# A hybrid gMLP and dilated-attention block: another order of the units in each half of the input projection

## Chip, cores and metric

One core of one Trainium2 chip. The metric is the device time of one execution in microseconds (us); every time below is a median of runs or a row of one profiled execution.

## The reference

`x` has 2048 tokens of 1024 features, in fp32. It is normalised and projected to nine groups of 1024 columns (gate_logits is two), which feed two branches:

```python
h = rmsnorm(x, g_norm)
proj = h @ w_in
a_u, a_v, a_gate, q, k, v, b_gate, gate_logits = jnp.split(proj, splits, axis=-1)
y_a = chunked_spatial_gating(gelu(a_u), gelu(a_v), w_s, b_s, g_v) * silu(a_gate)
y_b = dilated_attention(q, k, v) * silu(b_gate)
g_a, g_b = jnp.split(sigmoid(gate_logits), 2, axis=-1)
merged = g_a * (y_a @ w_proj_a) + g_b * (y_b @ w_proj_b)
return rmsnorm(x + merged @ w_out, g_final)
```

Column groups are told here by short names: u, av, g (branch A: a_u, a_v, a_gate), k, q, v, bg (b_gate), ga and gb (the two halves of gate_logits).

## The kernel before

**Precision.** Each fp32 operand is split in a high part (a cast, fp32r) and a low part (the rest, fp32r), and each product of a tile is three matmuls: hi x hi, hi x lo, lo x hi (`mm3`, L103). For weights ACT makes the high part (L83) and, from the end of the first V unit on, POOL the low part (L86); for the input ACT makes the high part (L144) and DVE or POOL the low part (L145).

**Halves and quarters.** Tokens are handled in two halves (`hf`) of 1024, each of two quarters (`qd`) of 512. X is the split, normalised input, 8 chunks of 128 features per quarter. `stats(qd)` (L155) loads 4 blocks of rows of x into two buffers ("xr", L161), squares and sums them on ACT (L162), scales on DVE (L77), takes the power -0.5 on POOL (L78), spreads the result over all partitions with four matmuls (L167), and ACT copies it to `rsbc` (L170). `h_chunk` (L147) then loads a chunk of x transposed and multiplies it by `rsbc` on DVE (L151). Four buffers ("ht") hold such chunks.

**Seven products.** Most units multiply blocks of a half as a 2 x 2 matrix with seven products (Strassen). They need input differences: T1 to T3 (`make_T`, L186: three loaded chunks, three DVE differences L196 to L200, the low parts on POOL) and T4 (`make_T4`, L204: DVE L212 and L213). T4 lies where part of X lay; `restore` makes that part again, from new loads. Weights go through a ring of 8 buffers; raw weights have two buffers.

**Units.** `unit_rows` is V of the first half; `ev_v` empties its banks (POOL fills ones, L447; ACT L451; DVE L452; a DMA). `unit_SR` makes outputs by rows (v of the second half and av): 2 blocks of weights x 7 products x 2 banks of 24 matmuls of 128x256. `unit_S` makes outputs by columns (k, q, u, g, bg, ga): 4 blocks of weights x 7 products of 12 matmuls of 128x512. `unit_P` is a plain product for one quarter, 8 banks of 24 matmuls of 128x512 (gb). `branch_a` runs u and g in turn.

**Scales.** k and q are stored in fp16 with a scale per group of columns. `scales_ahead` (L251) is a generator: 16 steps, each with a load of 128x1024 weights (`wrow`, in the "xr" buffers) and a DVE reduce (L262, with a running maximum, L265); then POOL's `partition_all_reduce` (L269) and three DVE steps. Calls of `next` set between which pieces of work it stands.

**Order.** A scheduler takes the program's text as priority and places each instruction on its engine's queue when its own model says that it is ready; each engine then runs its queue in order, and DMAs are issued from SP's. So a piece of text further down can stand earlier on an engine. First half: X of quarter 0, V, X of quarter 1 within V, T, T4, av with the scales among it, k, q, u and g, then bg, ga, restore. Second half: gate unit P0 on the old half's quarter 0 (still in X), X of quarter 2, statistics of quarter 3, gate unit P1 (old quarter 1), restore, T, T4, v, av, k, q, u, g, restore. Attention and the projections follow and are not touched.

Of the kernel before, what the change touches and what calls it, by code (L numbers as in the profile page):

```python
# [27 lines left out]
class Prog:  # L28
# [141 lines left out]
        nc.scalar.copy(bc, ps)  # L170
        self.bc[qd % 2] = bc

    def make_h(self, hp, qd):
        self.stats(hp, qd)
        X = self.alloc_X(qd % 2)
        for k in range(KC):
            self.split_X(X, k, self.h_chunk(hp, "ht", 4, qd, k))
        return X
# [568 lines left out]
    def window(self, at, fill, total_fill):  # L747
# [35 lines left out]
        for j in range(n + 3):  # L783
            if j < n:
                G = groups[j]
                h, p, g = G["h"], G["p"], G["g"]
                if g == 3 and j + 1 < n:
                    q = j // 4 + 1
                    vt[q // 3, 2 - q % 3] = self.load_v(at, q // 3, 2 - q % 3)
                if g == 0:  # L790
                    if p == 2:
                        OC = at.tile([P, 3, 16, 66], F32, name="OC", tag="OC", bufs=1)
                    if p == 1 and h + 1 < NH:
                        raw[h + 1] = self.load_qk(at, h + 1)
                if g == 0:
                    O = OC[:, 0] if p == 0 else at.tile([P, 16, 66], F32, name="ob", tag="ob", bufs=2)
                G.update(qk=self.qkp[p] if p else raw[h][:3], B=raw[h][3], V=vt[h, p], OC=OC, O=O)
                run(self.stage_s(at, G))

                nxt = {2: (h, 1), 0: (h + 1, 2)}.get(p)  # L800
                if nxt and nxt[0] < NH and g == 0:
                    perm = self.permuted(at, raw[nxt[0]], nxt[1])
                next(perm, None)
            if 2 <= j < n + 2:
                run(self.stage_t(at, groups[j - 2]))
            if j >= 3:
                G = groups[j - 3]
                run(self.stage_o(at, G))
                if G["p"] == 0 and G["g"] == 3:
                    pend.append(self.combine(at, G["h"], G["OC"]))  # L810
# [98 lines left out]
    def run(self):  # L909
        tc, io = self.tc, self.io  # L910
        self.setup()
        win = io["w_in"]
        self.pe = None

        def drain(g):
            for _ in g:
                pass
        self.bc = [None, None]

        def pool(name, **kw):  # L920
            return tc.tile_pool(name=name, **kw)
        with pool("tp", bufs=1) as self.tp, pool("wr", bufs=2) as self.wr, pool("cp", bufs=1) as self.cp:
            X = [None, None]
            for hf in range(2):
                qds = (2 * hf, 2 * hf + 1)
                with pool(f"hp{hf}", bufs=2) as hp:
                    rows = self.ev_v(hp, hf)
                    if hf == 0:
                        X[0] = self.make_h(hp, 0)
                        gen = self.unit_rows(X, win, 5120, rows, (0, 1), lambda wb: self.sv[:, wb:wb + 1])  # L930
                        next(gen)
                        X[1] = self.make_h(hp, 1)
                        drain(gen)
                        self.w_lo = self.nc.gpsimd
                    else:
                        drain(self.unit_P(X, win, 8192, self.ev_gate(self.gb_d), 0))
                        X0 = self.make_h(hp, 2)
                        self.stats(hp, 3)
                        drain(self.unit_P(X, win, 8192, self.ev_gate(self.gb_d), 1))
                        X = [X0, [None] * KC]  # L940
                        self.restore(X, 3, range(4, KC))
                    self.make_T(hp, qds)
                    self.make_T4(X)
                    if hf == 1:
                        drain(self.unit_SR(hp, X, win, 5120, rows))
                    ahead = self.scales_ahead(hp, win, (4096, 3072)) if hf == 0 else iter(())
                    for _ in self.unit_SR(hp, X, win, 1024, self.ev_av(hf)):
                        next(ahead, None)
                    drain(ahead)
                    if hf == 0:  # L950
                        self.scales()
                with pool(f"wq{hf}", bufs=2) as self.wq:
                    branch_a = self.branch_a(self.wq, hf, X)
                    next(branch_a)
                    for c0, dst, sc in ((4096, self.k_d, self.sk), (3072, self.q_d, self.sq)):
                        drain(self.unit_S(X, win, c0, self.ev_qk(dst, sc), qds))
                    drain(branch_a)
                if hf == 0:
                    drain(self.unit_S(X, win, 6144, self.ev_bg, qds))
                    drain(self.unit_S(X, win, 7168, self.ev_gate(self.ga_d), qds))  # L960
                self.restore(X, qds[1])
        self.wp = self.ctx.enter_context(pool("wp", bufs=2))
        self.every = 8
        self.w_hi = self.nc.gpsimd
        self.x_lo = self.nc.vector

        def fill():
            e = self.every
            yield from self.unit_T(X, win, 6144, self.ev_bg, (2, 3), every=e)
            yield from self.unit_T(X, win, 7168, self.ev_gate(self.ga_d), (2, 3), every=e)  # L970
            Y = [None, None]
            yield from self.unit_T(X, win, 8192, self.ev_gate(self.gb_d), (2,), every=e)
            Y[0] = self.load_X(0, self.ya_d)
            yield from self.unit_T(X, win, 8192, self.ev_gate(self.gb_d), (3,), every=e)
            for qd in range(4):
                if qd < 3:
                    Y[(qd + 1) % 2] = self.load_X(qd + 1, self.ya_d)
                yield from self.unit_T(Y, io["w_proj_a"], 0, self.ev_pa, (qd,), every=e)
        with tc.tile_pool(name="at", bufs=2) as at:
            self.window(at, fill(), 80 * 5.2)  # L980
        self.final()
# [48 lines left out]
```

## Time and profile before

| | |
|---|---|
| median of 3 runs | 2685.8 us (2683.05 to 2686.45) |
| the profiled execution's own time | 2690.79 us |
| its span in the trace | 2688.8 us |
| its mean granted TensorE clock | 0.974 |
| bg, ga and P0 (second half's first gate unit) | from about 560 to 758 us of the span |
| the first V unit's end, T4 and av's start | from about 100 to 200 us |
| the second V unit | from about 803 us |

A span is the time from the first to the last instruction in the trace; some 2 us of the run lie around it. In the rows further down, PE is TensorE's matmuls, PEld its weight loads, DVE VectorE, ACT ScalarE, POOL GpSimd and SP the engine that issues DMAs. "x12" counts instructions that a row holds together. An arrow "out<-in" names the tiles; wch and wcl are the two parts of a weight, wc both in one tile, pj, pt and ss are PSUM banks.

### The profile page before, as it was taken

What the parts mean: (1) busy time and instruction counts of PE and PEld (TensorE: products, weight loads), DVE (VectorE), ACT (ScalarE), POOL (GpSimd) and SP (SyncE); (2) the same over time, 40 slices, a digit from 0 to 9 for tenths busy, and PEclk for the clock granted to TensorE, in tenths of its full rate; (3) what the DMA queues carried; (4) which work ended last, traced back from release to release, by engine and by line L of the source; (5) the groups of instructions that cost most, each with busy time, mean ns of one, the idle gap of its engine ahead of it and who ended that gap; (6) DMA issues with size and microseconds to landing.
All of it is one profiled execution on the core that took longest, in us unless ns stands there. A gap on an engine that the chain in (4) does not pass through costs nothing.

```text
span 2688.8 us, 45128 instructions
## 1 busy us (share of the span) xinstructions
PE 2503.2 (93%) x16736; PEld 2122.7 (79%) x16736; DVE 1794.8 (67%) x3633; ACT 1255.1 (47%) x2481; POOL 888.2 (33%) x633
## 2 busy tenths in 40 slices
PE   5969999999998999999899899989889898899998
PEld 5969888888887898888677778878777777677787
DVE  5864767756258547677457877787989888545533
ACT  4335333343333353333257777676767665222221
POOL 0325554444444444544222222333333333000000
PEclk9989999999999999999899999999999999999999
DMA  7744333253453343323356646677777876755541
GB/s 232 162 126 142 102 118 106 94 171 116 153 167 89 87 138 115 122 95 114 99 142 158 185 127 181 177 195 201 200 217 194 237 206 176 239 168 184 169 132 63
DMA packets 463995, 410.00 MB, mean 152 GB/s; under 512 B 150432, under 2 KB 384288, under 8 KB 463776
## 3 DMA queue, kind: packets, MB, share of 16 engines
q1 hardware_dynamic: 463344, 407.05, 51.7%
q8 instruction: 132, 2.16, 0.3%
q14 instruction: 87, 0.71, 0.1%
q10 hardware_dynamic: 432, 0.07, 0.0%
HBM read 297.35 MB, written 109.71 MB: 151 GB/s over the span
## 4 chain that ended last, share of the span: by engine, by line
PE 67%; DVE 13%; DMA 10%; issue 4%; ACT 3%; POOL 1%; SPq 0%; ACTq 0%; DVEq 0%; POOLq 0%
PE pj L103 32%; PE pt L103 15%; PE ss L103 10%; PE pt L669 3%; DVE S L647 2%; PE ss L639 2%; DVE pl L673 1%; DVE X L145 1%; PE ss L640 1%; DMA v_d<-vst 1%; DMA wraw<-in_w_in 1%; DMA OC<-o_d 1%; DMA o_d<-ob 1%; PE pt L512 1%; DVE OC L727 1%
## 5 line engine op out<-in xcount | busy, mean ns | idle before, releaser
L103 PE MATMUL pj<-X,whi 128*128 128x512 f32 x1792 | 602.3, 411 | 16.5 <-POOL whi L85 11.1
L86 POOL TENSOR_TENSOR wc<-wraw,wc 128x512 fp32r<-128x512 f32 x240 | 327.4, 1372 | 318.7 <-ACT wc L83 307.2
L103 PEld LDWEIGHTS pj<-X,whi 128*128 128x128 f32 x1792 | 342.5, 195 | 88.1 <-POOL whi L85 12.0
L103 PE MATMUL pj<-X,wlo 128*128 128x512 f32 x896 | 369.2, 412 | 7.6 <-DVE wlo L86 4.0
L647 DVE CUSTOM_DVE_ANT_0 S<-ss,B,niqk 128x256 f32<-128x256 f32 (+1 forms) x768 | 284.3, 418 | 22.0 <-PE ss L640 21.8
L673 DVE SCALAR_TENSOR_TENSOR pl<-pt,ph 128x512 f16<-128x512 f32 x320 | 204.8, 653 | 93.3 <-ACT ph L672 92.0
L653 ACT ACTIVATE S<-S,ob 128x128 f32<-128x128 f32 (+1 forms) x512 | 193.4, 437 | 72.5 <-DVE ob L647 71.5
L83 ACT CAST wc<-wraw 128x512 fp32r<-128x512 f32 x240 | 145.2, 618 | 165.3 <-PE pt L103 78.8
L85 POOL TENSOR_SCALAR whi<-wraw 128x1024 fp32r<-128x1024 f32 x64 | 69.9, 1093 | 442.9 <-PE pj L103 393.2
L103 PEld LDWEIGHTS pj<-X,wlo 128*128 128x128 f32 x896 | 175.1, 195 | 46.5 <-DVE wlo L86 6.9
L672 ACT ACTIVATE ph<-pt 128x512 f16<-128x512 f32 x320 | 177.2, 565 | 61.1 <-PE pt L669 37.0
L103 PE MATMUL ss<-T,wc 128*128 128x512 f32 x768 | 188.2, 394 | 0.0
L103 PE MATMUL pt<-X,wc 128*128 128x512 f32 x768 | 185.2, 390 | 0.0
L103 PE MATMUL pj<-WO,X 128*128 128x512 f32 x768 | 180.7, 395 | 4.1 <-ACT X L872 3.9
L103 PEld LDWEIGHTS pj<-WO,X 128*128 128x128 f32 x768 | 144.2, 188 | 40.0 <-ACT X L872 5.2
L669 PE MATMUL pt<-ident,S 128*128 128x128 f32 x1200 | 168.6, 278 | 3.4 <-DVE pl L673 3.3
L86 POOL TENSOR_TENSOR wcl<-wraw,wch 128x1024 fp32r<-128x1024 f32 x52 | 129.2, 2486 | 121.4 <-ACT wch L83 97.2
L103 PEld LDWEIGHTS ss<-T,wc 128*128 128x128 f32 x768 | 143.6, 188 | 32.0
L103 PEld LDWEIGHTS pt<-X,wc 128*128 128x128 f32 x768 | 143.9, 188 | 30.3
L86 POOL TENSOR_TENSOR wlo<-wraw,whi 128x1024 fp32r<-128x1024 f32 x64 | 164.5, 2571 | 5.3
L103 PE MATMUL pt<-T,wc 128*128 128x512 f32 x672 | 165.0, 394 | 0.0
L669 PEld LDWEIGHTS pt<-ident,S 128*128 128x128 f32 x1200 | 141.7, 144 | 15.1 <-DVE pl L673 4.4
(229 smaller groups left out, 5777.8 us busy)
## 6 DMA issues: line engine op xcount, KB each, us to landing
wraw<-in_w_in SPq DMA_DIRECT2D x64, 1024.0 KB, 5.7
V<-v_d SPq DMA_DIRECT2D x48, 520.0 KB, 4.8
o_d<-ob SPq DMA_DIRECT2D x32, 528.0 KB, 5.1
OC<-o_d SPq DMA_DIRECT2D x32, 528.0 KB, 4.7
wraw<-in_w_in SPq DMA_DIRECT2D x32, 512.0 KB, 5.4
wraw<-in_w_proj_a SPq DMA_DIRECT2D x32, 512.0 KB, 5.3
wraw<-in_w_proj_b SPq DMA_DIRECT2D x32, 512.0 KB, 4.7
xt<-in_xT SPq DMA_DIRECT2D x60, 256.0 KB, 4.3
```

Source lines behind the costliest of these rows:

```text
L83: nc.scalar.copy(hi, raw)
L85: nc.gpsimd.tensor_scalar(out=hi, in0=raw, scalar1=1.0, scalar2=0.0, op0=ALU.mult, op1=ALU.add)
L86: self.w_lo.tensor_tensor(out=lo, in0=raw, in1=hi.bitcast(F32), op=ALU.subtract)
L103: self.pe = nc.tensor.matmul(out, st(a, k), mv(b, k), start=first and n == 0, stop=last and n == len(todo) - 1)
L145: self.x_lo.tensor_tensor(out=X[k][1], in0=src, in1=X[k][0].bitcast(F32), op=ALU.subtract)
L512: nc.tensor.matmul(px[:, i * P:(i + 1) * P], av[:, 4 * q + i], w, start=True, stop=True)
L639: nc.tensor.matmul(ps[:, i, :n], q, KH[:, w], start=True, stop=False)
L647: nc.vector.tensor_tensor_reduce(out=S[:, j, :n], in0=ps[:, i, :n], in1=B[:, bo:bo + n], scale=self.niqk[:, pr:pr + 1], scalar=3e38, op0=A ...
L653: nc.scalar.activation(S[:, i, :rng[i]], S[:, i, :rng[i]], AF.Exp, bias=ob[:, i, 65:66], scale=-1.0)
L669: self.pe = nc.tensor.transpose(px[:, j * P:(j + 1) * P], G["S"][:, i, c * P:(c + 1) * P], self.ident)
L672: nc.scalar.activation(ph[:, :n], px[:, :n], AF.Copy, scale=PSCALE)
L673: nc.vector.scalar_tensor_tensor(out=pl[:, :n], in0=px[:, :n], scalar=PSCALE, in1=ph[:, :n], op0=ALU.mult, op1=ALU.subtract)
```

## The change

bg and ga of the first half, which stood behind g, now stand ahead of av, right behind T4, and the text puts two steps of the scales behind each of their eight blocks. In the second half the text makes the statistics of quarter 2 ahead of P0, those of quarter 3 and the differences T behind it, and X of quarter 2 behind T (`make_h` is told not to make the statistics again); T4 is behind restore as before. The V unit of the second half now stands in the `else` arm.

```diff
-    def make_h(self, hp, qd):
-        self.stats(hp, qd)
+    def make_h(self, hp, qd, have=False):
+        if not have:
+            self.stats(hp, qd)
...
                         drain(gen)
                         self.w_lo = self.nc.gpsimd
+                        self.make_T(hp, qds)
+                        self.make_T4(X)
+                        ahead = self.scales_ahead(hp, win, (4096, 3072))
+                        for c0, ev in ((6144, self.ev_bg), (7168, self.ev_gate(self.ga_d))):
+                            for _ in self.unit_S(X, win, c0, ev, qds):
+                                next(ahead, None)
+                                next(ahead, None)
+                        drain(ahead)
                     else:
+                        self.stats(hp, 2)
                         drain(self.unit_P(X, win, 8192, self.ev_gate(self.gb_d), 0))
-                        X0 = self.make_h(hp, 2)
                         self.stats(hp, 3)
+                        self.make_T(hp, qds)
+                        X0 = self.make_h(hp, 2, True)
                         drain(self.unit_P(X, win, 8192, self.ev_gate(self.gb_d), 1))
                         X = [X0, [None] * KC]
                         self.restore(X, 3, range(4, KC))
-                    self.make_T(hp, qds)
-                    self.make_T4(X)
-                    if hf == 1:
+                        self.make_T4(X)
                         drain(self.unit_SR(hp, X, win, 5120, rows))
-                    ahead = self.scales_ahead(hp, win, (4096, 3072)) if hf == 0 else iter(())
-                    for _ in self.unit_SR(hp, X, win, 1024, self.ev_av(hf)):
-                        next(ahead, None)
-                    drain(ahead)
+                    drain(self.unit_SR(hp, X, win, 1024, self.ev_av(hf)))
...
                     drain(branch_a)
-                if hf == 0:
-                    drain(self.unit_S(X, win, 6144, self.ev_bg, qds))
-                    drain(self.unit_S(X, win, 7168, self.ev_gate(self.ga_d), qds))
                 self.restore(X, qds[1])
```

Line numbers of the changed kernel are one higher from about L174 on (the memset L447 is L448, the all-reduce L269 is L270).

**POOL behind the first V unit.** The rows run from the last T difference on. Before, the low parts are those of av's weights (128x1024, wcl):

```order
L145 TENSOR_TENSOR T_3_1_1331<-xt,T_3_0_1330 128x512
L447 MEMSET vst 128x8x2 x3
L86 TENSOR_TENSOR wcl<-wraw_1449,wch 128x1024
L86 TENSOR_TENSOR wcl<-s1w,wch 128x1024
L269 ISA
L269 ISA wra<-wma 128x17
L86 ISA
L86 TENSOR_TENSOR wcl<-wraw_1451,wch 128x1024
```

Of the change, where they are those of bg's weights (128x512, wc); two more, of its first two weights, stand a few rows ahead:

```order
L145 TENSOR_TENSOR T_3_1_1331<-xt,T_3_0_1330 128x512
L86 TENSOR_TENSOR wc<-wraw_1448,wc 128x512
L86 TENSOR_TENSOR wc<-s_1456,wc 128x512
L448 MEMSET vst 128x8x2 x3
L270 ISA
L270 ISA wra<-wma 128x17
L86 ISA
L86 TENSOR_TENSOR wc<-wraw_1448,wc 128x512 x3
L86 TENSOR_TENSOR wc<-wraw_1604,wc 128x512 x3
```

The all-reduce keeps its place behind the last three memsets of V; four low parts of bg's first block are ahead of it and three behind. On DVE the sixteen reduces still stand among V's evacuations in both.

**PE and DVE where the second half begins.** Before, L167 for the statistics of quarters 2 and 3 stands behind all 8 banks of P0 (`pj` is its last bank, `pt` the first of P1):

```order
L103 MATMUL pj<-X_7_0_211,wch 128x512
L103 MATMUL pj<-X_7_1_212,wch 128x512
L103 MATMUL pj<-X_7_0_211,wcl 128x512
L167 MATMUL pt<-ident,rs 128x128 x8
L103 MATMUL pt<-X_0_0_6203,wch 128x512
```

Of the change, four of them stand behind the third of P0's banks; the other four matmuls (quarter 3) stand behind P0's last bank, where all eight stood:

```order
L103 MATMUL pj<-X_7_0_211,wch 128x512
L103 MATMUL pj<-X_7_1_212,wch 128x512
L103 MATMUL pj<-X_7_0_211,wcl 128x512
L167 MATMUL pt<-ident,rs 128x128 x4
L103 MATMUL pt<-X_0_0_197,wch 128x512
```

DVE of the change at g's last outputs (`tg` is an output of g; X_0 to X_3 are the restored part), where before these rows of X stood behind ga:

```order
L523 SCALAR_TENSOR_TENSOR tg<-tg,u_6128 128x512
L145 TENSOR_TENSOR X_0_1_6204<-xt,X_0_0_6203 128x512
L524 SCALAR_TENSOR_TENSOR tg<-tg,um 128x512
L364 TENSOR_TENSOR u_6079<-ss,u_6079 128x512
L145 TENSOR_TENSOR X_1_1_6211<-xt,X_1_0_6210 128x512
L145 TENSOR_TENSOR X_2_1_6218<-xt,X_2_0_6217 128x512
L523 SCALAR_TENSOR_TENSOR tg<-tg,u_6079 128x512
L151 SCALAR_TENSOR_TENSOR xt<-xt,gn,rsbc 128x512
L524 SCALAR_TENSOR_TENSOR tg<-tg,um 128x512
L145 TENSOR_TENSOR X_3_1_6225<-xt,X_3_0_6224 128x512
L77 TENSOR_SCALAR ss<-ss 128x4
```

**DVE during P1.** Before, X of quarter 2 (here its last chunk) and then the differences (L196 to L200):

```order
L145 TENSOR_TENSOR X_6_1_6534<-xt,X_6_0_6533 128x512
L151 SCALAR_TENSOR_TENSOR xt<-xt,gn,rsbc 128x512 x3
L145 TENSOR_TENSOR X_7_1_6536<-xt,X_7_0_6535 128x512
L151 SCALAR_TENSOR_TENSOR xt<-xt,gn,rsbc 128x512 x2
L196 TENSOR_TENSOR xt<-xt 128x512
L198 TENSOR_TENSOR xt<-xt 128x512
L200 TENSOR_TENSOR xt<-xt 128x512
```

Of the change, the last differences, then X, with the sums of the V unit's weights (L286, L287) among its first chunks:

```order
L199 TENSOR_TENSOR xt<-xt 128x512
L201 TENSOR_TENSOR xt<-xt 128x512
L145 TENSOR_TENSOR X_0_1_6641<-xt,X_0_0_6640 128x512
L286 TENSOR_TENSOR s1w<-wraw_7026 128x1024
L151 SCALAR_TENSOR_TENSOR xt<-xt,gn,rsbc 128x512
L287 TENSOR_TENSOR wraw_7026<-wraw_7024,wraw_7026 128x1024
L145 TENSOR_TENSOR X_1_1_6643<-xt,X_1_0_6642 128x512
L151 SCALAR_TENSOR_TENSOR xt<-xt,gn,rsbc 128x512 x3
L145 TENSOR_TENSOR X_2_1_6645<-xt,X_2_0_6644 128x512
L145 TENSOR_TENSOR X_3_1_6647<-xt,X_3_0_6646 128x512
```

The two have changed places; the multiplications by `rsbc` (L151) run ahead of both by up to four chunks.

## The prediction

> **What bounds the kernel now.** I read the page's head first, then its chain of work that ended last, then busy time in windows of the three places that the change touches.
>
> ```profile
> span 2688.8 us, 45128 instructions
> PE 2503.2 (93%) x16736; PEld 2122.7 (79%) x16736; DVE 1794.8 (67%) x3633; ACT 1255.1 (47%) x2481; POOL 888.2 (33%) x633
> PE 67%; DVE 13%; DMA 10%; issue 4%; ACT 3%; POOL 1%; SPq 0%; ACTq 0%; DVEq 0%; POOLq 0%
> 100.00:200.00 100.00, 77.10 (x603) 76.21 (x602) 72.30 (x92) 30.69 (x60) 35.31 (x25) 0.88 0.56 140
> 555.00:765.00 210.00, 210.00 (x928) 172.52 (x927) 91.97 (x121) 85.31 (x139) 99.36 (x67) 1.00 0.46 153
> 800.00:960.00 160.00, 141.13 (x1080) 138.06 (x1079) 112.20 (x125) 56.61 (x103) 67.68 (x43) 0.95 0.39 99
> ```
>
> PE is busy 93% of the span, so a change that adds and removes no matmul can only move PE's idle time and its slow clock. The window rows (length, then busy time of PE, PEld, DVE, ACT, POOL, granted clock, DMA) say where these are: 22.9 us idle in 100 to 200, none in 555 to 765, where bg, ga and the second half's first gate unit run, and 18.9 us in 800 to 960. The question is what becomes of these three places.
>
> **First place: behind the V unit.** PE's timeline (start, length, instruction; in brackets the idle time before it and its releaser) and the chain:
>
> ```profile
> 128.71 0.28 PE L103 MATMUL pj<-wch,X 128*128 128x256 f32 x1
> 139.02 0.35 PE L103 MATMUL pt<-wch,X 128*128 128x256 f32 x1 [1.51 <-DVE vst L452]
> 155.74 0.58 PE L103 MATMUL pj<-wch,T 128*128 128x256 f32 x1 [13.62 <-ACT wch L83]
> 177.50 0.58 PE L103 MATMUL pt<-wcl,T 128*128 128x256 f32 x1 [5.92 <-POOL wcl L86]
> 158.16 4.67 PE pj L103 x23
> 177.50 5.18 PE pt L103 x23
> 182.68 2.85 PE ss L103 x24
> 259.20 2.72 PE pt L103 x12
> ```
>
> The V unit ends at 128.71, where av's first bank begins. By 182.68 av has nine banks of 24 matmuls done; a bank at the full clock takes 2.88 (2.85 in the row), so 54.0 - 9 x 2.88 = 28.1 us are lost. About 4 of these are slow clock: the banks behind the two long gaps took 4.67 and 5.18 for 23 matmuls.
>
> In the changed program bg's first block stands here, whose products are one bank of 12 matmuls, 2.72 each (the S product at 259.20). What does not move is the run of scales: by DVE's rows in the new order its 16 reduces still stand among V's evacuations, and POOL's all-reduce stands ahead of the low parts of bg's weights 4 to 6.
>
> ```profile
> 135.13 1.21 DVE L262 TENSOR_REDUCE wma<-wrow 128x8 f32<-128x1024 f32 x1
> 159.07 1.22 DVE L262 TENSOR_REDUCE wmr<-wrow 128x8 f32<-128x1024 f32 x1 [0.94 <-DMA wrow<-in_w_in]
> 165.91 0.15 DVE L265 TENSOR_TENSOR wma<-wma,wmr 128x8 f32<-128x8 f32 x1
> 166.33 0.42 POOL L269 PARTITION_ALL_REDUCE wra<-wma  x1 [5.88 <-DVE wma L265]
> 175.12 4.67 POOL L86 TENSOR_TENSOR wcl<-wraw,wch 128x1024 fp32r<-128x1024 f32 x2 [8.37 <-issue]
> L86 POOL TENSOR_TENSOR wc<-wraw,wc 128x512 fp32r<-128x512 f32 x240 | 327.4, 1372 | 318.7 <-ACT wc L83 307.2
> ```
>
> The ninth reduce (a new wma) comes at 135.13 and the sixteenth ends at 160.3, paced by loads into two buffers and not by PE. Its maximum could follow at 160.5; before, T4's work on DVE held it to 165.9. POOL then takes 0.42 for the all-reduce and stays 8.37 in "issue" before its next subtraction, and one low part of 128x512 takes 1.37. So weight 4 is ready between 160.5 + 0.42 + 8.37 + 1.37 = 170.7 and 5.5 later, and I take 171, since the new order has the maximum close behind its reduce. PE will have done four products, 10.9 us, by about 140 and then **waits some 30 us**: 171 - 128.7 - 10.9 = 31.4 lost, and 2 of slow clock behind it (4.67 - 2.85 above). 33.4 against 28.1 makes **+5**. Ends: -4, if the last load lands early and the 8.37 shrinks, and +10, if T4 holds the maximum back as before.
>
> The 8.37 is the term that I cannot see into. The Trainium skill, GPSIMD Engine Reference, section on instruction dispatch, says that the first call into a freshly loaded library pays about 6 us of code load that the profile does not show. The trace agrees that such a gap is there, with 8.37 in place of 6; by the page's figure this term would be +3, an estimate.
>
> **Second place: the start of the second half.** Before, the statistics of quarter 2 were issued when the gate unit g of branch A ended, and bg and ga (150 us of PE without a gap, by the window 555 to 765) covered them. Now P0 stands right behind g, and the matmul of these statistics (L167) stands on PE behind P0's third bank, so it is due 3 x 5.44 = 16.3 us after g ends.
>
> ```profile
> 560.29 2.72 PE pj L103 x12
> 560.86 0.69 DVE L363 TENSOR_TENSOR u<-ss,u 128x512 f32<-128x512 f32 x1
> 577.25 1.06 ACT L162 ACTIVATE xr<-xr 128x1024 f32<-128x1024 f32 x1 [1.28 <-DMA xr<-in_x]
> 578.43 0.17 DVE L77 TENSOR_SCALAR ss<-ss 128x4 f32<-128x4 f32 x1 [2.35 <-ACT xr L162]
> 14.09 1.03 POOL L78 TENSOR_TENSOR rs<-ss,mhalf 128x4 f32<-128x4 f32 x1 [13.21 <-DVE ss L77]
> 720.02 5.44 PE pt L103 x24
> 777.76 0.68 DVE L145 TENSOR_TENSOR X<-xt,X 128x512 fp32r<-128x512 f32 x1
> ```
>
> In the trace g ends at 560.3 and L77 comes 18.1 later, because the x loads stand on SP behind g's last output and use two buffers. In the new order three low parts of X (0.68 each, the row at 777.76) and one more sum stand among g's last DVE rows, +2.8 on that output and on the loads behind it. L77 then comes 20.9 after g, the power 1.0 later: 21.9 against 16.3, a gap of 5.5 us and about 1 of slow clock, **+6.5**. Ends: 0, if the loads run ahead of the output, and +10. The second set of statistics has another 20 us before P0 ends and costs nothing.
>
> **Third place: the second half's V unit.** L167 of quarter 3 still stands behind P0's last bank, as before, and all that needs its broadcast starts there in both programs.
>
> ```profile
> 757.94 1.95 PE L167 MATMUL pt<-ident,rs 128*128 128x128 f32 x16
> 760.02 3.33 DVE L151 SCALAR_TENSOR_TENSOR xt<-xt,gn,rsbc 128x512 f32<-128x512 f32 x3 [39.64 <-ACT rsbc L170]
> 819.41 1.78 DVE L200 TENSOR_TENSOR xt<-xt 128x512 f32<-128x512 f32 x1
> 845.72 2.88 DVE L145 TENSOR_TENSOR T<-td,T 128x512 fp32r<-128x512 f32 x1
> 132.97 2.24 DVE wraw L289
> 813.78 0.49 PE L103 MATMUL pj<-wcl,X 128*128 128x256 f32 x1 [4.46 <-POOL wcl L86]
> 823.46 0.39 PE L103 MATMUL ss<-wcl,T 128*128 128x256 f32 x1 [2.18 <-POOL wcl L86]
> 841.36 0.38 PE L103 MATMUL pj<-wch,T 128*128 128x256 f32 x1 [1.94 <-DVE c L310]
> 845.30 0.39 PE L103 MATMUL pt<-wcl,X 128*128 128x256 f32 x1 [0.71 <-POOL wcl L86]
> 850.45 0.39 PE L103 MATMUL ss<-wch,X 128*128 128x256 f32 x1 [2.13 <-DVE u L310]
> ```
>
> The work is 8 chunks of X (760 to 778) and 12 of differences (778 to 821), 61 us on DVE, SP, ACT and POOL together, and T4 behind them to 848.6. P1, eight banks, covers only 8 x 5.44 = 43.5 of the 61. Before, X came first: it lay ready at 778, well ahead of the V unit, whose first products need X and whose later ones need T; the gaps were 4.46 + 2.18 + 1.94 + 0.71 + 2.13 = 11.4 us and some 3.5 of slow clock, my estimate at 1.8 for each of the two longest (4.67 - 2.85, as above). The new rows put the differences first. They take 821 - 778 = 43 us and end about when P1 does, 44.5 behind 757.94 (43.5 and 1.0 of L167). X's eight chunks follow at 2.3 each ((778 - 760)/8) with two weight sums of V (2.24, the row of L289) among the first four. X chunks 0 to 3, which the first product needs, are there 43 + 4 x 2.3 + 4.5 = 57 us behind 757.94: 12.5 late. Chunks 4 to 7 are ready 7 us later, as three of their first steps stand ahead by then, while the first product takes 2 x 2.88: 1.2 more. So 13.7 us and 3 of slow clock stand in place of 11.4 and 3.5, **+2**. Ends: -11, if X is ready with P1 and only some 4 us of the old waits stay, and +8, if X's first four chunks take the 3.6 us each that those of the differences took (43/12).
>
> **What costs nothing.** bg's and ga's other blocks do the same products on the same weights as between 555 and 710, where PE never waited; ga to av is now an S to SR passage with the weights in the ring. No load is added or removed.
>
> **The sum.** 5 + 6.5 + 2 = 13.5 us on the profiled execution, which took 2690.8 (span 2688.8 and 2.0 around it), 5.0 above the median of the three runs. On the median 2685.8 this is 2699; as each term's lower side is the wider one I take **2698**.
>
> **Rivals.**
> (a) *Faster: the differences hidden under P1.* If the loads and DVE work of the differences were to run during P0's and P1's matmuls as their place in the code suggests, the 15 us of the third place would go, and with the first two terms near nothing the time would be near 2671. Against it stands the order: the broadcast of quarter 3, which every difference needs, still comes from L167 at P0's end. The case is decided where X's chunk 3 is ready before P1 ends, 12.5 us sooner than I work out.
> (b) *The places cancel, or the change does not do what it says.* The reduces stay in V's time, so "scales among bg and ga" is empty, and the statistics may come in time: with +5, 0 and the third place 4 better (the waits of 2.18 and 1.94, both of products that read differences, are gone), about 2687.
> (c) *Slower still: the all-reduce pays a code load.*
>
> ```profile
> 24.22 1.33 POOL L245 PARTITION_ALL_REDUCE wr<-wm  x1 [9.11 <-DVE wcl L86]
> ```
>
> At 24.22 POOL was 9.11 idle ahead of the all-reduce. A second such wait at the first place, with the maximum held to 166, gives +14 there and 2708 in all.
>
> **How the numbers follow.** Forecast +6 to +20: 0.50; (a) 0.17; (b) 0.20; (c) 0.13. For this kernel 0.2%, 5.4 us, is about what a measurement can tell from no change. Forecast and (c) are slower, 0.63; (b) is the same, 0.20; (a) is faster, 0.17. The range, 2677 to 2712, or -9 to +26, takes in the forecast, (b) and (c) and the near part of (a); the terms' upper ends, +10, +10 and +8, sum to 28, and what it leaves out, most of (a), is under 2 in 10.
>
> **What would show it.** First place: one PE gap of about 30 us, from 140 on, ahead of a product that reads T and wc, released by POOL, with the all-reduce just before. Without it the term is wrong. Second: a gap of 5 us ahead of L167 sixteen us behind g's end, released by POOL's rs. Third: a gap of about 12 us ahead of the first V product, released by DVE's or ACT's X, and no wait for the differences later. The forecast falls if X is ready with P1, or if the all-reduce comes before the last V evacuation.

## The result

The changed kernel took 2702.5 us in the median of 4 runs (2698.0 to 2705.9), against 2686.1 of the kernel before: a ratio of 1.0062 with a 95% interval of 1.0045 to 1.0080. A second comparison (e5 below), beside which the kernel before took 2695.4, gave 1.0059 (1.0038 to 1.0081). So the change costs some 16 us. Single runs of one kernel spread over 10 us or more, and most of that lies behind the part that the change touches: from the first attention matmul to the end the traces of this study take between 1313 and 1329 us, with the same work in all.

The page's head of the profiled execution, and the windows of the three places (length, busy time of PE, PEld, DVE, ACT and POOL, granted clock, DMA share, GB/s):

```profile
span 2696.2 us, 45128 instructions
PE 2502.7 (93%) x16736; PEld 2118.9 (79%) x16736; DVE 1788.4 (66%) x3633; ACT 1256.1 (47%) x2481; POOL 892.9 (33%) x633
...
PE 68%; DVE 13%; DMA 10%; issue 4%; ACT 3%; POOL 2%; SPq 1%; DVEq 0%; POOLq 0%; ACTq 0%
```

```profile
100.00:200.00 100.00, 72.72 (x403) 62.82 (x403) 70.49 (x103) 28.57 (x55) 38.83 (x36) 0.85 0.56 141
560.00:770.00 210.00, 202.31 (x937) 167.74 (x936) 118.36 (x159) 76.66 (x122) 90.38 (x60) 0.98 0.43 138
800.00:960.00 160.00, 140.07 (x1038) 133.79 (x1037) 113.45 (x128) 58.94 (x99) 76.97 (x44) 0.95 0.43 113
```

PE's work is the same to 0.5 us. Its idle time in 100 to 200 went from 22.9 to 27.3; the stretch where the second half begins, which had none, has 7.7; in 800 to 960 it is 19.9 in place of 18.9. These are PE's waits over 1.6 us in the timeline of the changed kernel up to the V unit's fourth bank, with the first product behind the first V unit ahead of them; the second broadcast (771.40) and the first mixing matmul (1164.90) are shown as marks. The trace has two records for each of the broadcast matmuls in the queue, so four of them read x8:

```profile
126.48 2.91 PE L103 MATMUL pj<-X,wc 128*128 128x512 f32 x12
137.31 4.57 PE L103 MATMUL pt<-T,wc 128*128 128x512 f32 x12 [2.40 <-DVE wma L266]
151.45 1.22 PE L103 MATMUL pj<-T,wc 128*128 128x512 f32 x2 [9.58 <-ACT wc L83]
167.98 4.61 PE L103 MATMUL pj<-T,wc 128*128 128x512 f32 x10 [15.31 <-POOL wc L86]
740.74 2.08 PE L167 MATMUL pt<-ident,rs 128*128 128x128 f32 x8 [7.46 <-POOL rs L78]
771.40 1.05 PE L167 MATMUL pt<-ident,rs 128*128 128x128 f32 x8
817.75 0.38 PE L103 MATMUL ss<-wch,X 128*128 128x256 f32 x1 [1.63 <-ACT wch L83]
822.12 0.58 PE L103 MATMUL ss<-wcl,X 128*128 128x256 f32 x1 [3.98 <-POOL wcl L86]
827.89 0.58 PE L103 MATMUL ss<-wch,X 128*128 128x256 f32 x1 [2.90 <-ACT X L144]
1164.90 1.05 PE L513 MATMUL pt<-wst,avg 128*128 128x128 f32 x8
```

To tell the places apart I divide each trace at three rows that every kernel has: the end of the first V unit (126.48 here, 128.71 before), the start of P0, and the first mixing matmul of the second half (L513 above, 1164.90). P0's start is worked back from the broadcast matmul: it stands behind three banks of 5.44, so 740.74 - 7.46 - 16.32 = 716.96; before, behind eight, 757.94 - 43.52 = 714.42. Waits of 0.15 to 0.60 us inside those banks, in the changed kernel, e4, e5 and e7, are left out of this. The row for the mixing matmul before:

```profile
1153.21 1.05 PE L512 MATMUL pt<-wst,avg 128*128 128x128 f32 x8
```

V's end to P0 took 590.5 us in place of 585.7, **4.8 more**, and P0 to the mixing matmul 447.9 in place of 438.8, **9.1 more**; 13.9 in all. The second trace of the changed kernel (e5) has 593.0 and 449.0, 17.5 in all. The mean of the two, 15.7, is near what the runs show, so the two stretches are enough to account for it. That a later stage has no part in it is not shown: behind the mixing matmul the two traces of this one kernel take 1531 and 1546 us, and the one of before 1536. The recorded expectations below count from the span's start, where the lag is 2.5 us at P0 and 11.7 at the mixing matmul, since the V unit happened to end 2.2 us sooner in the first trace of the change.

### The profile page after: what moved, and what is told of

Same layout as the page of the kernel before. It is cut to its first block, busy times and chain, and to the rows that moved or that the text cites. A ratio compares the mean times of both kernels' runs of the same rounds, so it can differ in the third digit from the quotient of the medians.

```text
span 2696.2 us, 45128 instructions
## 1 busy us (share of the span) xinstructions
PE 2502.7 (93%) x16736; PEld 2118.9 (79%) x16736; DVE 1788.4 (66%) x3633; ACT 1256.1 (47%) x2481; POOL 892.9 (33%) x633
## 4 chain that ended last, share of the span: by engine, by line
PE 68%; DVE 13%; DMA 10%; issue 4%; ACT 3%; POOL 2%; SPq 1%; DVEq 0%; POOLq 0%; ACTq 0%
PE pj L103 32%; PE pt L103 16%; PE ss L103 10%; PE pt L670 3%; DVE S L648 2%; PE ss L640 2%; PE ss L641 1%; DMA OC<-o_d 1%; DVE pl L674 1%; DVE X L145 1%; DVE OC L728 1%; DMA xr<-in_x 1%; PE pt L513 1%; DMA xt<-in_xT 1%; DMA wraw<-in_w_in 1%
## 5 line engine op out<-in xcount | busy, mean ns | idle before, releaser
L103 PE MATMUL pj<-X,whi 128*128 128x512 f32 x1792 | 599.4, 409 | 16.5 <-POOL whi L85 12.1
L103 PEld LDWEIGHTS pj<-X,whi 128*128 128x128 f32 x1792 | 341.6, 194 | 87.2 <-POOL whi L85 12.9
L83 ACT CAST wc<-wraw 128x512 fp32r<-128x512 f32 x240 | 145.0, 617 | 171.5 <-PE pt L103 77.2
L86 POOL TENSOR_TENSOR wcl<-wraw,wch 128x1024 fp32r<-128x1024 f32 x52 | 135.6, 2609 | 132.8 <-ACT wch L83 103.1
```

Source lines behind the costliest of these rows:

```text
L83: nc.scalar.copy(hi, raw)
L86: self.w_lo.tensor_tensor(out=lo, in0=raw, in1=hi.bitcast(F32), op=ALU.subtract)
L103: self.pe = nc.tensor.matmul(out, st(a, k), mv(b, k), start=first and n == 0, stop=last and n == len(todo) - 1)
```

## The experiments

Each of e1 to e10 ran in five rounds beside the kernel before. In this table all times are taken as above (columns two to four in us, from one trace each). P0's start is worked back from the first broadcast behind it: over three banks and the wait for the changed kernel, e4, e5 and e7, over five banks for e8 and e10, and over eight for the others (in e2, whose first broadcast stands ahead of P0, from the second); outside the first group PE has no wait ahead of that broadcast.

| kernel | V's end to P0 | P0 to mixing matmul | sum against before | ratio of runs, 95% interval |
|---|---|---|---|---|
| before | 585.7 | 438.8 | 0 | 1 |
| changed | 590.5 | 447.9 | +13.9 | 1.0062 (1.0045 to 1.0080) |
| e5 changed, again | 593.0 | 449.0 | +17.5 | 1.0059 (1.0038 to 1.0081) |
| e1 first half alone | 592.3 | 436.7 | +4.5 | 1.0010 (0.9994 to 1.0025) |
| e2 second half alone | 585.9 | 440.3 | +1.7 | 0.9996 (0.9980 to 1.0011) |
| e3 statistics early | 595.8 | 440.5 | +11.8 | 1.0022 (1.0010 to 1.0034) |
| e4 scales held | 581.5 | 448.9 | +5.9 | 1.0005 (0.9988 to 1.0021) |
| e6 statistics held | 590.6 | 439.0 | +5.1 | 1.0020 (1.0008 to 1.0031) |
| e7 all-reduce late | 583.1 | 450.1 | +8.7 | 1.0021 (1.0007 to 1.0034) |
| e8 all of these | 574.6 | 433.5 | -16.5 | 0.9933 (0.9915 to 0.9951) |
| e9 first half of e8 | 573.6 | 437.4 | -13.5 | 0.9926 (0.9906 to 0.9946) |
| e10 second half of e8 | 585.7 | 431.7 | -7.1 | 0.9957 (0.9940 to 0.9974) |

The two traces of the changed kernel differ by 2.5 us at the first place; the runs tell totals to some 4 us. A single trace can also be an extreme one: the traces of e3, e5 and e7 are of the slowest run of their kernel, the first of the changed kernel and that of e2 of the fastest.

### e1 and e2: each half of the change alone

e1 has the first half's new order and the old `else` arm; e2 the new `else` arm and the old first half.

Of e1, against the changed kernel:

```diff
-                        self.stats(hp, 2)
                         drain(self.unit_P(X, win, 8192, self.ev_gate(self.gb_d), 0))
+                        X0 = self.make_h(hp, 2)
                         self.stats(hp, 3)
-                        self.make_T(hp, qds)
-                        X0 = self.make_h(hp, 2, True)
...
+                        self.make_T(hp, qds)
```

Of e2, against the changed kernel:

```diff
-                        for c0, ev in ((6144, self.ev_bg), (7168, self.ev_gate(self.ga_d))):
...
+                    for _ in self.unit_SR(hp, X, win, 1024, self.ev_av(hf)):
+                        next(ahead, None)
...
+                    drain(self.unit_S(X, win, 6144, self.ev_bg, qds))
+                    drain(self.unit_S(X, win, 7168, self.ev_gate(self.ga_d), qds))
```

> Only the first half of the change: bg and ga ahead of av, the second half in the old order. Theory A (the time of the change is the sum of three places: first V unit, start of the second half, second V unit, which in the trace lag by 2.6, about 8 and about 1 us): only the first place is left, so about 2.6 us over before, near 2689; PE waits of some 27 us between 130 and 168 us as in the changed kernel, no wait ahead of the broadcast matmuls of the statistics (they stand behind all of P0, 43 us after g, and were ready 22 and 36 us after g). Rival B (the median is 16 us up while the three places give 12, so some of it comes from a later stage or from running bg and ga early): 2694 or more.

> Only the second half of the change: statistics and differences in the new order, bg and ga of the first half behind g as before. Theory A: bg and ga cover the statistics of quarter 2 again, so the wait of 7.5 us ahead of the broadcast matmul is gone, and the new order of differences and X costs about 1 us: 2685 to 2689. Rival D (the differences ahead of X are themselves what costs, since X comes late for the first product of v): 2694 or more, with waits of over 15 us in the second V unit.

e1 pays 4.5 us and e2 1.7 by the trace, and neither can be told from before by its runs; rival B, 8 us or more for e1, lies outside the interval of e1's ratio and falls. Together they would be 6; the changed kernel pays 14 to 17. The rest, 8 to 11, is paid by neither half alone: it is the wait for quarter 2's statistics, which arises only where bg and ga are gone from between g and P0 *and* the broadcast has been put among P0's banks. In e1 it stands behind P0 and finds its input ready; in e2 bg and ga cover it. Rival D falls: with the differences ahead of X, P0 to the mixing matmul takes 1.5 us more than before, 2.5 if before is counted without the broadcast that e2 makes ahead of P0, and not 10.

### e5: the changed kernel again

> The changed kernel again, since single runs of one kernel spread over 10 us or more and the first comparison had four. Theory A (the change costs the projections 11.7 us and nothing after them): a ratio of 1.003 to 1.005 and the same three waits as in the first trace, within 2 us each. Rival B (it costs 16 us or more, part of it in a later stage): 1.006 or more. Rival H (the first comparison was drawn from the upper end, and the projections' lag is mostly made good later): 1.002 or less.

The ratio came out above the band of theory A and just under that of rival B. In the trace the first place costs more (7.3 us, with a wait of 12.56 in place of 9.58), and the sum is 17.5, so no later stage is needed for it; the spread behind the mixing matmul is too wide to exclude one. The two traces bracket the loss that the runs show. The wait that ends with ACT's fifth high part, behind V's last outputs, differs between traces with the same work there (9.58, 12.56, 11.86 in e1 and 13.22 in e6), and it stays when the all-reduce is gone, as e7 shows.

### e3 and e6: quarter 2's statistics in the first half

Of e6, against the changed kernel; e3 has the call of `stats` without the line ahead of it:

```diff
-                        self.stats(hp, 2)
                         drain(self.unit_P(X, win, 8192, self.ev_gate(self.gb_d), 0))
...
                     if hf == 0:
+                        with tc.issue_after(self.last_w):
+                            self.stats(hp, 2)
                         self.scales()
```

`last_w` is the latest load of raw weights on SP; `issue_after` places what is issued on that engine behind it.

> The changed kernel with the statistics of quarter 2 made at the end of the first half's av (their broadcast takes the place of quarter 0's, which nothing reads after the differences). Theory A: the wait of 7.5 us ahead of the broadcast matmul goes and nothing takes its place: 8 us under the changed kernel, near 2694.5. Rival E (P0 is late for another reason too, its weights or the restored X, so that the wait turns up at another place): within 3 us of the changed kernel, 2699 to 2703, with new waits in P0.

> The changed kernel with quarter 2's statistics made in the first half's av, and their loads held on SP behind av's last weights, so that they cannot stand in the first V unit as they did in the run before. Theory A: the waits behind the first V unit are those of the changed kernel (25 to 29 us), the wait ahead of the broadcast matmul is gone, the second half's first mixing matmul comes 8 us sooner than in the changed kernel (about 1157), and the time is 8 us under it. Rival E (P0 waits for something else): 1162 or later.

In both, PE has no wait ahead of a broadcast matmul, and P0 to the mixing matmul takes 439.0 to 440.5, as before: rival E falls. But e3 gives much of it back at the first place. Its text stands behind av, yet the loads were issued from 150 us on, behind the last rows of the scales, and on ACT the square of the first block came to stand ahead of the high part (L83) that PE waits for. ACT's timeline and then PE's, of e3:

```profile
150.51 1.12 ACT L144 CAST T<-td 128x512 fp32r<-128x512 f32 x2
155.00 1.06 ACT L162 ACTIVATE xr<-xr 128x1024 f32<-128x1024 f32 x1 [3.36 <-DMA xr<-in_x]
...
156.05 1.12 ACT L83 CAST wc<-wraw 128x512 fp32r<-128x512 f32 x2
```

```profile
137.36 3.02 PE L103 MATMUL pt<-T,wc 128*128 128x512 f32 x12 [1.53 <-DVE wma L266]
156.71 1.22 PE L103 MATMUL pj<-T,wc 128*128 128x512 f32 x2 [16.33 <-ACT wc L83]
173.29 4.63 PE L103 MATMUL pj<-T,wc 128*128 128x512 f32 x10 [15.37 <-POOL wc L86]
```

ACT stands 3.36 us for a load that nothing needed yet, and the cast that the changed kernel made at 150.8 comes at 156.1. This is what one trace shows, of the slowest of e3's 12 runs; by the runs e3 and e6 cannot be told apart (1.0022 and 1.0020). With the loads held (e6) the first place costs what it does in the changed kernel, 4.9 over before, and the second nothing. So the second place is worth 8.9 us of the 13.9 (447.9 - 439.0).

### e4 and e7: what holds PE behind the first V unit

e4 holds the loads of the scales behind bg's and ga's weights; e7 holds only the last step, the all-reduce, behind av's first low parts on POOL (`last_lo`).

Of e4, against the changed kernel:

```diff
                             for _ in self.unit_S(X, win, c0, ev, qds):
-                                next(ahead, None)
-                                next(ahead, None)
+                            for m, _ in enumerate(self.unit_S(X, win, c0, ev, qds)):
+                                if c0 == 7168 or m > 1:
+                                    for _ in range(3):
+                                        with tc.issue_after(self.last_w):
+                                            next(ahead, None)
```

Of e7:

```diff
-                        drain(ahead)
...
+                        if hf == 0 and n == 0:
+                            with tc.issue_after(self.last_lo):
+                                drain(ahead)
```

> The changed kernel with each load of the scales' weight rows queued on SP behind the latest load of bg's or ga's weights, from bg's third block on, three steps per block, so that the reduces and the all-reduce fall among bg and ga, as the words of the change say. Theory A (the all-reduce ahead of bg's fifth low part holds PE for 15.3 us, and the reduces among V's evacuations hold the rest): the waits of 27 us behind the first V unit fall to 12 or less, and the time by 15 or more: 2687 or lower. Rival F (V's evacuation through two buffers and its DMAs holds the fifth weight anyway): the waits fall by 5 at most, 2697 or more. Rival G (the all-reduce holds PE in ga instead): a new wait of about 8 us in ga, 2694.

> The changed kernel with only the all-reduce of the scales (and what follows it) held behind av's first low parts on POOL; the reduces and their loads stay where they were, among V's evacuations. Theory A (the wait of 15.3 us is POOL's, which stands at the all-reduce and then 8 us behind it before its next subtraction): the 15.3 goes but for 2 us, the wait for ACT's fifth high part (9.6) stays, and the mark comes 13 us sooner than in the changed kernel, about 1152. Rival I (the reduces among V's evacuations are the cause, and the all-reduce only the last in line): waits of 20 us or more stay behind the first V unit.

e7's wait of 15.3 is gone, and what stays is 3.32 + 11.05 + 0.68 + 2.10 = 17.2 us (timeline of e7). The mark came at 1161.8, only 3 us sooner than in the changed kernel, where theory A had 13: the V unit ended 2.1 us later in this trace, the second half took 2.2 longer, the waits of 3.32 and 11.05 are 2.4 longer than their counterparts, and PE's matmuls up to P0 took 2.2 longer (565.4 us busy in place of 563.2). By the table e7 gains 5.2 us on the first trace of the changed kernel, by the runs some 10.

```profile
141.18 5.46 PE L104 MATMUL pt<-T,wc 128*128 128x512 f32 x12 [3.32 <-DVE wma L267]
157.69 2.58 PE L104 MATMUL pj<-T,wc 128*128 128x512 f32 x4 [11.05 <-ACT wc L83]
167.43 2.55 PE L104 MATMUL ss<-T,wc 128*128 128x512 f32 x10 [0.68 <-DVE vst L454]
172.07 0.73 PE L104 MATMUL ss<-T,wc 128*128 128x512 f32 x2 [2.10 <-DVE T L146]
```

So the place has two causes in series. Rival I, which had 20 us or more, is right for its part: what stays is V's evacuation with the scales' reduces on DVE and their loads among it; e4 shows what they add. In the changed kernel POOL's timeline shows both causes:

```profile
143.77 0.11 POOL L448 MEMSET vst<- 128x16 f16 x1 [11.13 <-DMA v_d<-vst]
151.12 0.11 POOL L448 MEMSET vst<- 128x16 f16 x1 [7.24 <-DMA v_d<-vst]
158.25 0.42 POOL L270 PARTITION_ALL_REDUCE wra<-wma  x1 [7.02 <-DVE T L145]
166.66 6.20 POOL L86 TENSOR_TENSOR wc<-wraw,wc 128x512 fp32r<-128x512 f32 x5 [7.99 <-issue]
```

V's last banks leave through two buffers, each free for POOL's next memset when its DMA has landed (11.13 and 7.24 us of waiting), and ACT's high part of bg's fifth weight stands behind their evacuation. Then, from the last memset at 151.2 to the low part at 166.7, POOL is taken by the all-reduce for 15.4 us, as long as PE's wait of 15.31. DVE's last maximum ended at 153.5 in that trace:

```profile
153.34 0.17 DVE L266 TENSOR_TENSOR wma<-wma,wmr 128x8 f32<-128x8 f32 x1
```

so for most of the 7.02 the all-reduce's input lay ready. The T row that stands as releaser is no input of it. In e1, e3, e5 and e6 it likewise starts 6.6 to 7.1 us behind the memset, and 3.8 to 5.1 behind the last maximum. In e7 the maximum was ready at 159.0, and the all-reduce at 336.31 still starts 7.76 behind the low part ahead of it:

```profile
336.31 0.42 POOL L271 PARTITION_ALL_REDUCE wra<-wma  x1 [7.76 <-issue]
```

That both sides of an all-reduce cost about 8 us shows where no input is waited for, in the same trace during V:

```profile
56.73 0.37 POOL L246 PARTITION_ALL_REDUCE wr<-wm  x1 [8.13 <-issue]
58.89 1.30 POOL L246 PARTITION_ALL_REDUCE wr<-wm  x1 [1.78 <-DVE wm L244]
63.81 0.11 POOL L448 MEMSET vst<- 128x16 f16 x1 [3.62 <-DMA v_d<-vst]
68.04 0.65 POOL L246 PARTITION_ALL_REDUCE wr<-wm  x1 [4.12 <-DVE wm L244]
76.82 1.53 POOL L145 TENSOR_TENSOR T<-xt,T 128x512 fp32r<-128x512 f32 x1 [8.14 <-issue]
```

Ahead of the first all-reduce POOL stands 8.13 us, from it to the next only 1.78, and from the last of three to a subtraction 8.14. The memset between the second and the third has waits of 3.62 and 4.12 beside it, for a store and for an input; in e4 a memset follows an all-reduce with no gap at all (84.66 and 84.91). So a memset does not pay the way out. Spans on POOL are rough, so that a part of this may be the all-reduce itself; the starts of its neighbours are what counts.

In e4, with loads and reduces gone too, the waits behind V are 0.61 + 1.61 + 4.29 + 0.68 = 7.2 us, and V's end to P0 falls 9.0 under the changed kernel. That is less than the 20.1 us by which these waits shrink: 8.6 come back as waits in bg and ga, and PE's matmuls take 2.5 longer (565.7 us busy in place of 563.2). In all e4 gains 8.0 on the changed kernel by the trace and some 15 by the ratio of the runs, where theory A had 15. Rival F falls. Rival G is right about part of the remainder: the all-reduce, now in ga, holds a product there for 5.84 us (PE and POOL of e4):

```profile
272.82 4.63 PE L103 MATMUL pt<-T,wc 128*128 128x512 f32 x10 [5.84 <-POOL wc L86]
```

```profile
264.15 0.42 POOL L271 PARTITION_ALL_REDUCE wra<-wma  x1 [5.88 <-DVE c L365]
271.51 1.25 POOL L86 TENSOR_TENSOR wc<-s,wc 128x512 fp32r<-128x512 f32 x1 [6.94 <-issue]
```

### e8: all places at once

e4's hold of the loads (with the steps counted so that the sixteen end in ga and the all-reduce is left for av), e7's hold of the all-reduce, e6's statistics, and quarter 3's statistics issued behind P0's fifth bank. Of the last, against the changed kernel, whose line for quarter 2 is gone too:

```diff
-                        drain(self.unit_P(X, win, 8192, self.ev_gate(self.gb_d), 0))
-                        self.stats(hp, 3)
+                        for n, _ in enumerate(self.unit_P(X, win, 8192, self.ev_gate(self.gb_d), 0)):
+                            if n == 4:
+                                with tc.issue_after(getattr(self.pe, "ins", self.pe)):
+                                    self.stats(hp, 3)
```

> All three places at once: the loads of the scales held behind bg's and ga's weights, the all-reduce held behind av's first low parts, quarter 2's statistics held behind av's last weights, and quarter 3's broadcast matmul behind the fifth bank of P0 in place of the eighth, so that the differences start 16 us sooner. Theory A (three places, each as worked out): waits of 8 us or less behind the first V unit, none ahead of the broadcasts, under 4 us in the second V unit; the mark near 1128 to 1135, 20 us or more before that of the kernel before, and the time 20 us under it. Rival J (one of them comes back: the loads held back crowd the DMAs of bg and ga, or the second V unit waits for its weights and not for X): a mark of 1145 or later, with the new wait in the trace.

The mark came at 1134.6 and the runs at 0.9933, 18 us under before, a little short of theory A's 20. Behind the first V unit the waits are 1.62 + 4.53 + 0.80 + 0.31 = 7.3 us, and there is none ahead of a broadcast. In the second V unit they are more than the 4 us forecast (2.13, 1.56, 1.97 and 3.45 are the longest), and P1 has two new ones, of 2.87 and 1.37, for low parts of its weights: something of rival J, though not to its mark of 1145. The two windows that had the most idle time:

```profile
100.00:200.00 100.00, 91.20 (x490) 77.37 (x490) 73.42 (x96) 34.47 (x66) 48.33 (x40) 0.97 0.56 150
800.00:960.00 160.00, 147.09 (x1193) 145.45 (x1192) 100.00 (x118) 64.61 (x127) 65.87 (x40) 0.98 0.40 102
```

8.8 us of PE idle in the first in place of 27.3, at a granted clock of 0.97 in place of 0.85, and 12.9 in the second in place of 19.9 (the unit begins earlier in e8, so that this window holds a little more of what follows it). The all-reduce now stands in av, where its trip costs PE 0.87 us (POOL and PE of e8):

```profile
314.24 2.40 POOL L86 TENSOR_TENSOR wcl<-wraw,wch 128x1024 fp32r<-128x1024 f32 x1 [3.28 <-ACT wch L83]
326.38 0.41 POOL L272 PARTITION_ALL_REDUCE wra<-wma  x1 [9.74 <-issue]
334.62 4.72 POOL L86 TENSOR_TENSOR wcl<-wraw,wch 128x1024 fp32r<-128x1024 f32 x2 [7.82 <-ACT junk L482]
```

```profile
337.04 0.39 PE L104 MATMUL pj<-wcl,X 128*128 128x256 f32 x1 [0.87 <-POOL wcl L86]
```

### e9 and e10: each half of e8 alone

e9 has e8's first half and the `else` arm of before. e10 has the first half of before and e8's `else` arm, with the statistics of quarter 2 held as in e6.

Of e9, against e8:

```diff
-                        for n, _ in enumerate(self.unit_P(X, win, 8192, self.ev_gate(self.gb_d), 0)):
-                            if n == 4:
-                                with tc.issue_after(getattr(self.pe, "ins", self.pe)):
-                                    self.stats(hp, 3)
-                        self.make_T(hp, qds)
-                        X0 = self.make_h(hp, 2, True)
+                        drain(self.unit_P(X, win, 8192, self.ev_gate(self.gb_d), 0))
+                        X0 = self.make_h(hp, 2)
+                        self.stats(hp, 3)
```

> Only the first half of the fastest kernel so far: bg and ga ahead of av with the scales' loads and the all-reduce held as there; the second half in the order of before. From the end of the first V unit P0 starts 585.7 us later before, 590.5 in the changed kernel and 574.6 in the fastest. Theory A (the first place alone makes that difference): 573 to 577, no wait ahead of the statistics' broadcasts (their loads run during P0 and the matmuls stand at its end), the second half as before (438.8 us from P0 to its first mixing matmul), in all 10 to 12 us under before. Rival K (the statistics, with nothing between g and P0 to cover them, delay the second V unit): over 443 us from P0 to that matmul, 5 us under before or less.

> Only the second half of the fastest kernel so far: the first half in the order of before (bg and ga behind g, scales among av), quarter 2's statistics held behind av's last weights, quarter 3's broadcast behind the fifth bank of P0, differences ahead of X. Theory A (the second half's part of the gain does not need the new place of bg and ga): P0 to the first mixing matmul 433 to 436 us in place of 438.8, first half as before, so 3 to 6 us under before. Rival L (the gain of the second half comes only with bg and ga gone from there): 438 us or more, no gain.

e9's first place gains 12.1 us and its second half stands as before; rival K falls. e10 gains 7.1, all behind P0, without bg and ga in a new place; rival L falls, and the gain is somewhat over theory A's band of 3 to 6. By the runs e9 and e8 can't be told apart (0.9926 and 0.9933, the intervals nearly the same); by the trace e8 is 3 us ahead. The runs of e9 and e10 gain more than their traces say (20 and 12 us by the ratios), and e8 does not gain the sum of both; why is left open. So the new place of bg and ga together with the holds is worth some 12 us by the trace, and the new place alone costs 5 to 7. What the holds would give in the old order, with bg and ga behind g and the scales held back among later units, was not run, so how the 12 us divide between place and holds stays open.

## Why the prediction was right

The forecast was 2698 (2677 to 2712) and slower; the runs gave 2702.5, and 13.9 to 17.5 us by two traces where the sum was 13.5.

**First place, +5: right in size, half right in mechanism.** It came to +4.8, +7.3 and, in e1, +6.6. The predicted wait of some 30 us from 140 on, ahead of a product that reads T and wc, with the all-reduce in POOL's queue, is there as 2.40 + 9.58 + 15.31 = 27.3. But the step that has the sixteenth reduce set its end ("the sixteenth ends at 160.3, paced by loads into two buffers and not by PE") failed: that reduce's maximum was done at 153.5 (of the 7 us between the two, 2.2 are the V unit's earlier end in this trace), and the all-reduce waited for POOL itself, which turned to it behind V's last memset and took 7.0 us to get there. The chain is the store that frees the buffer for V's last memset, 7.0 in, 0.42, 8.0 out, 1.3 for the low part. That the size came out is luck: a maximum forecast 7 us too late made up for a way into the all-reduce that had no cost. Rival (c) had the row for that cost (9.11 ahead of the all-reduce at 24.22), but as an unlikely extra; it is the rule. The Trainium skill, GPSIMD Engine Reference, section on instruction dispatch, gives about 6 us for the first call to a freshly loaded kernel, which was weighed for the gap behind the all-reduce; the rows at 56.73 and 76.82 have 8.1 on both sides. The order of the queue, read ahead of the run, showed rightly that the reduces would not move.

**Second place, +6.5: right in place and cause, too small.** The wait stood where it was forecast, behind P0's third bank, released by POOL's power, 7.46 and 5.87 us in the two traces against 5.5. The slow clock behind it was underrated: from the one broadcast to the next five banks should take 27.2 and took 30.66 with the 1.0 of broadcast matmuls that before ran at P0's end, so 2.5 us went to a slow clock (0.50 granted from 741 to 745) where about 1 was forecast. By e6 the place is worth 8.9.

**Third place, +2: right in size on the mean of the traces, but not made up as forecast.** From the second broadcast to the mixing matmul took 393.5 us (1164.90 - 771.40) against 395.3 before (1153.21 - 757.94, with 1.0 of broadcast matmuls that now stand elsewhere), so -0.8; by the same measure e2, where this order alone is changed, has +2.5, e6 +1.2 and e5 +2.6. The seven traces with the differences ahead of X and quarter 3's broadcast at P0's end have a mean of 395.6 and the three with the old order 393.1 without the 1.0, which makes +2.5; PE's idle time in this stretch is 19.9 to 23.8 us in the former and 18.9 to 19.4 in the latter. The differences ended 44 us behind the broadcast, for 43 forecast, and X's chunk 3 came 58 to 59 behind it, for 57. What was mis-sized is the wait made of it, "12.5 late": the first product did not wait for its four chunks together but began with chunk 0 at 816 and took the others as they came, and its waits sum to 1.63 + 3.98 + 0.40 + 0.29 + 2.90 + 0.48 = 9.7 us in place of 13.7, and further waits come later in the unit, where the sum had none (1.87 at 864.25, for an output's sum). The 3.98 is a wait for a low part of its weights, which no step had.

**What cost nothing** cost nothing: from 200 to 560 us PE had no wait over 0.3 us in the changed kernel.

Rival (a) named the right condition: with the differences ahead of X and nothing else nothing is gained (e2), and with quarter 3's broadcast at P0's fifth bank 7 us are (e10). Of rival (b) the first condition held (the reduces stayed in V's time), and the second, statistics in time, did not; its time fits either half of the change alone (e1 and e2).

## What to carry to other kernels

Read from the queues, not from the text, where moved work will stand: the scales' loads went into the first V unit wherever the text put them, until they were held behind a load that can't be issued earlier. Before a stage is taken from between two others, ask what it covered: here 150 us of matmuls hid a chain of loads, sums and a power that is 22 to 25 us long (16.3 and the waits of 5.87 to 8.32), and the two halves of the change were each nearly free and cost 9 us only together. An operation that costs its engine a way in and a way out, as the all-reduce does on POOL, belongs where that engine's next results are not needed for as long: in e8 POOL goes from one low part through the all-reduce to the next in 18.0 us (316.6 to 334.6), and PE waits 0.87 for it.

## What the runs showed of the hardware

POOL's change between its subtractions and the all-reduce costs about as much in each direction, by the rows at 56.73 and 76.82; a memset behind an all-reduce does not pay it (84.91 in e4). What POOL does in that time the traces do not show. In its queue one instruction without tiles (ISA) stands ahead of the all-reduce and one ahead of the next low part, which fits, but that the time is theirs is not shown. Where an input arrives meanwhile, the way in shows as a wait for that input. How long each way takes varies: in, it was 5.88 in e4, 7.02 in the first trace of the changed kernel and 9.74 in e8; out, 6.94, 7.99 and 7.82, and 11.39 in e3.
